# One-hot matrices of the second keys kept in DRAM between two halves of an expert layer, and a new split of the row gathers

## The chip, the cores and the metric

The kernel runs on one core of a Trainium2 chip. The metric is the device time of one execution in microseconds, lower is better. A measurement is the median of several runs.

## What is computed

A trunk of two layers over 512 tokens of width 1024. Each layer has a mixer (gMLP gating beside stick-breaking attention), which the change does not touch, and then PEER: each token picks 8 x 16 of 16384 single-neuron experts by two sets of 128 sub-keys and adds their outputs. Cut to that part:

```python
s1 = jnp.einsum('phd,kd->phk', q[:, :, 0], k1); s2 = jnp.einsum('phd,kd->phk', q[:, :, 1], k2)
v1, i1 = lax.top_k(s1, 16); v2, i2 = lax.top_k(s2, 16)
...                                   # top 16 of the pair sums
eid = jnp.take_along_axis(i1 * 128 + i2, top_pos, axis=-1)
g = jax.nn.softmax(top_s, axis=-1)
act = jax.nn.gelu(jnp.einsum('pd,phkd->phk', xb, u_tab[eid]))
return jnp.einsum('phk,phkd->pd', g * act, v_tab[eid])
```

## The kernel before

**Two ways through the experts.** Tokens 0 to 383 (ND = 384) are computed densely: for each of the 128 blocks of 128 experts (block b holds the experts with first key b) TensorE multiplies the whole block. The last 128 tokens are computed by gathers: for each of 128 picks, one indirect DMA fetches a row of `u` for each token, VectorE takes its dot product with the token (L825), and later 128 gathers of `v` rows are added up with their weights (L833). That is 256 gathers of 512 KB a layer. Each gather has one of three buffers `grow_` (L820 on): GpSimd may issue gather n+3 only when VectorE is done with gather n.

**Items and stages.** A *u item* is 24 matmuls of 384 columns (L128 to L130, into one of two PSUM banks `u0`, `u1`, which alternate from item to item), then a gelu on ScalarE (L536 and L539). A *v item* is 18 matmuls of 512 columns into `acc`. `PLAN` at the top of the file sets four stages: 32 u items (blocks 32 to 63; the first 32 blocks run earlier, beside other work), 64 v items, 64 u items, 64 v items. They are called **u1, v1, u2 and v2** here. PLAN also gives each stage its gathers: 2, 100, 64, and the rest, 90.

**One-hots.** The routing weights are made dense by matmuls. For 16 tokens at a time, `onehots(c, tg)` builds on VectorE `oa`, the one-hot of the second key (L758), `om`, that of the first key in the half c (L761), and `ob`, `om` times the weight in two parts (L765). Then `spread` (L773, L774) multiplies `oa` by `ob`, 8 tokens (16 short matmuls) at a time, and `weigh` moves the result to SBUF: VectorE L788 where the gelu of the block is known, ScalarE L790 where not. There are 24 such groups in u1 (c = 0) and the same 24 again in u2 (c = 1); `oa` does not depend on c. In u2 a spread writes into the `u` bank that the u item before it has used, so it has to wait until ScalarE has read that bank (L536, L539).

**Order.** All of this is under a manual schedule: each engine works through its instructions in the order in which the code is written. `run` calls, for the item i of a stage, `meanwhile(i)` when two of its eight k steps (six matmuls) are issued:

```python
fresh = [spread(*hot.pop(0)) for _ in range(steps[i][1])]
while late: late.pop(0)()
for part in fresh: weigh(*part)
...
if todo and len(hot) <= TG // TB and ...: hot.extend(onehots(*todo.pop(0)))
due = min(steps[i][2], len(left))
if due: gather(left.pop(0))
prepare(i + LOOK)
for _ in range(due - 1): gather(left.pop(0))
```

`prepare(i + 2)` loads the weights of the item after the next: a DMA on SyncE's queue (L121) into one of two buffers `raw` (u items) or one of the pool `wide` (v items), a copy to `hi` on ScalarE (L114), and `lo` = raw - hi on VectorE (L117). The item's own gelu on ScalarE comes behind this `hi`. The pool `wide` has four buffers of 512 KB; in u1 and u2 they hold two pairs of `oa` and `ob`.

Of the kernel before, what the change touches and what calls it, by code (L numbers as in the profile page):

```python
# [10 lines left out]
F32 = mybir.dt.float32  # L11
F32R = mybir.dt.float32r
F16 = mybir.dt.float16
# [4 lines left out]
OP = mybir.AluOpType  # L18
# [3 lines left out]
P = 128  # L22
L = 2
S = 512
D = 1024
KD = D // P
NTT = S // P
NDT = 3
ND = NDT * P
GT = 3  # L30
NH = 8
NK = 128
# [5 lines left out]
CH = NK // 2  # L38
NS2 = 11
NS1 = CH - NS2  # L40
TG = 16
SUB = 2
# [17 lines left out]
HEAD = 1  # L60
MID = 2
PLAN = [("u", range(FIRST, CH), 1, 2),
        ("v", [*range(NS1, CH), *range(NS1)], 0, 100),
        ("u", range(CH, NK), 1, 64),
        ("v", range(CH, NK), 0, 2 * P)]


# [1 line left out]
def trunk(ctx: ExitStack, tc: tile.TileContext, x, rows1, rows2, ada, w_qk, w_row, w_o, wq, kt, wst,  # L69
          vnorm, fnorm, ut, u_rows, v_rows, out):  # L70
    nc = tc.nc
    V, A, G, T = nc.vector, nc.scalar, nc.gpsimd, nc.tensor
# [1 line left out]
    cp = ctx.enter_context(tc.tile_pool(name="const", bufs=1))  # L74
    st = ctx.enter_context(tc.tile_pool(name="stream", bufs=2))

    xd = ctx.enter_context(tc.tile_pool(name="xd", bufs=1, space=bass.MemoryType.DRAM)).tile([NTT, P, D], F32, name="xd")
    held = {}

    def open_xs():  # L80
# [412 lines left out]
    def peer(l):  # L493
        with tc.tile_pool(name="pe", bufs=1) as pe, \
# [7 lines left out]
            i2t = pe.tile([P, ND], F16, name="i2t")  # L502
# [229 lines left out]
            with tc.tile_pool(name="gp", bufs=1) as gp, ExitStack() as psc:  # L732
                iot = gp.tile([P, P, SUB], F16, name="iot")
# [17 lines left out]
                def by_key(rows, n):  # L751

                    return rows.rearrange("p (g i) -> p g i", i=SUB)[:, :, None, :].to_broadcast([P, TG // SUB, n, SUB])

                def onehots(c, tg):
                    ts = slice(tg * TG, (tg + 1) * TG)
                    oa = gp.tile([P, TG // SUB, P, SUB], F16, name="wide", bufs=4)
                    V.tensor_tensor(oa, iot[:, None].to_broadcast([P, TG // SUB, P, SUB]), by_key(i2t[:, ts], P),  # L758
                                    OP.is_equal)
                    m = gp.tile([P, TG // SUB, CH, SUB], F16, name="om", bufs=1)  # L760
                    V.tensor_tensor(m, iot[:, None, c * CH:(c + 1) * CH].to_broadcast([P, TG // SUB, CH, SUB]),  # L761
                                    by_key(i1t[:, ts], CH), OP.is_equal)
                    ob = gp.tile([P, 2, TG // SUB, CH, SUB], F16, name="wide", bufs=4)
                    for part in range(2):
                        V.tensor_tensor(ob[:, part], m, by_key(gt[:, part, ts], CH), OP.mult)  # L765
                    return [(c, tg * TG + q * TB, oa, ob) for q in range(TG // TB)]
# [73 lines left out]
                def run(steps):  # L840
# [6 lines left out]
                    def meanwhile(i):  # L847
                        fresh = [spread(*hot.pop(0)) for _ in range(steps[i][1])]
                        while late:
                            late.pop(0)()  # L850
                        for part in fresh:
                            weigh(*part)
                        if i + 1 < len(steps) and len(steps[i + 1][0]) > 2:
                            close[i + 1] = steps[i + 1][0][2]()
                        if todo and len(hot) <= TG // TB and todo[0][0] <= steps[min(i + 1, len(steps) - 1)][4]:
                            hot.extend(onehots(*todo.pop(0)))
                        due = min(steps[i][2], len(left))
                        if due:
                            gather(left.pop(0))
                        prepare(i + LOOK)  # L860
                        for _ in range(due - 1):
                            gather(left.pop(0))

                    for i in range(LOOK):
                        prepare(i)
                    hot.extend(onehots(*todo.pop(0)))
                    for i in range(len(steps)):
                        w = ready.pop(i) + close.pop(i, ())
# [20 lines left out]
                for side, bs, spreads, gathers in PLAN:  # L889
                    items = [(u_item if side == "u" else v_item)(b) for b in bs]  # L890
                    chunk += spreads
                    n, g0, n0 = len(items), 0, 0
# [89 lines left out]
```

## Time and profile before

| | |
|---|---|
| median of 3 runs | 3146.86 us (3141.15 to 3151.80) |
| profiled execution, its own time | 3151.26 us |
| its span | 3149.6 us |
| TensorE matmul busy | 2988.5 us, 95% |
| VectorE busy | 2485.8 us, 79% |
| ScalarE busy | 1167.8 us, 37% |
| GpSimd busy | 798.6 us, 25% |
| u2 in the first layer | about 1010 to 1318 us |
| u2 in the second layer | about 2554 to 2858 us |

Busy shares are means over stages with different limits, so the stages are read one by one: how long a stage took, how many matmuls it held, and how long the same matmuls take in a stretch without a wait. The ends of matmuls in the records are modelled, so the pace is read from their starts and counts.

### The profile page before, as it was taken

How to read it: one execution, taken by the hardware profiler on the slowest of the kernel's cores; microseconds unless marked ns; L12 is line 12 of the kernel's file. 1: busy time of each engine (PE TensorE's matmuls, PEld its weight loads, DVE VectorE, ACT ScalarE, POOL GpSimd, SP SyncE). 2: the span in 40 equal slices, each digit the busy share in tenths (PEclk: the TensorE clock that was granted, in tenths of full speed). 3: DMA queues.
4: the chain of work that ended last, by engine and by line, in shares of the span. 5: the costliest groups of instructions: out<-in, count | busy, mean ns of one | idle time of the engine just before them, and what ended most of it. 6: DMA issues, size and time to landing. Idle time of an engine off the chain costs nothing. (4 is left out here: it accounts for less than half of the span.)

```text
span 3149.6 us, 47135 instructions
## 1 busy us (share of the span) xinstructions
PE 2988.5 (95%) x17532; PEld 2612.1 (83%) x17532; DVE 2485.8 (79%) x4951; ACT 1167.8 (37%) x2016; POOL 798.6 (25%) x584
## 2 busy tenths in 40 slices
PE   5988999999999999999999999999999999999998
PEld 4777888998777999977778888889987789998776
DVE  7687798797778889777853558969887888997787
ACT  3263333333333433333343633324333334333332
POOL 0000000003545323244500000000055543333452
PEclk8999999999999999999999999999999999999999
DMA  8746233337888666688832032333388876667885
GB/s 301 253 159 208 88 101 113 109 108 257 304 305 283 248 215 238 228 313 302 287 117 94 3 107 90 105 114 114 129 307 307 306 268 235 227 233 271 320 304 202
DMA packets 178840, 651.45 MB, mean 207 GB/s; under 512 B 19850, under 2 KB 20274, under 8 KB 178610
## 3 DMA queue, kind: packets, MB, share of 16 engines
q1 hardware_dynamic: 104018, 378.14, 35.8%
q0 software_dynamic: 73728, 268.47, 22.7%
q8 instruction: 137, 2.24, 0.3%
q10 hardware_dynamic: 864, 1.84, 0.2%
q14 instruction: 93, 0.76, 0.1%
HBM read 642.08 MB, written 6.29 MB: 206 GB/s over the span
## 5 line engine op out<-in xcount | busy, mean ns | idle before, releaser
L128 PE MATMUL u<-hh,hi 128*128 128x384 f32 x1920 | 665.1, 346 | 20.1 <-ACT act L539 17.3
L130 PE MATMUL u<-hh,lo 128*128 128x384 f32 x1920 | 648.2, 338 | 5.5 <-DVE lo L117 5.5
L129 PE MATMUL u<-hl,hi 128*128 128x384 f32 x1920 | 647.2, 337 | 0.0
L130 PE MATMUL acc<-hi,hl 128*128 128x512 f32 x1536 | 607.8, 396 | 32.8 <-DVE hl L117 32.5
L129 PE MATMUL acc<-lo,hh 128*128 128x512 f32 x1536 | 602.8, 392 | 7.0 <-DVE lo L117 6.9
L128 PE MATMUL acc<-hi,hh 128*128 128x512 f32 x1536 | 601.1, 391 | 0.0
L117 DVE TENSOR_TENSOR lo<-raw,hi 128x1024 fp32r<-128x1024 f32 x350 | 426.6, 1221 | 193.3 <-ACT hi L114 192.5
L114 ACT ACTIVATE hi<-raw 128x1024 fp32r<-128x1024 f32 x352 | 372.5, 1059 | 521.4 <-PE b L129 132.1
L114 ACT ACTIVATE hh<-act 128x384 fp32r<-128x384 f32 x256 | 134.4, 525 | 680.6 <-PE acc L129 677.5
L128 PEld LDWEIGHTS u<-hh,hi 128*128 128x128 f32 x1920 | 363.9, 190 | 24.7 <-ACT act L539 18.6
L130 PEld LDWEIGHTS acc<-hi,hl 128*128 128x128 f32 x1536 | 289.5, 188 | 113.3 <-DVE hl L117 54.3
L130 PEld LDWEIGHTS u<-hh,lo 128*128 128x128 f32 x1920 | 363.5, 189 | 6.6 <-DVE lo L117 6.6
L129 PEld LDWEIGHTS u<-hl,hi 128*128 128x128 f32 x1920 | 364.4, 190 | 1.4
L129 PEld LDWEIGHTS acc<-lo,hh 128*128 128x128 f32 x1536 | 289.7, 189 | 75.3 <-DVE lo L117 15.1
L128 PEld LDWEIGHTS acc<-hi,hh 128*128 128x128 f32 x1536 | 289.9, 189 | 57.9
L117 DVE TENSOR_TENSOR lo<-wide,hi 128x1024 fp32r<-128x1024 f32 x232 | 283.0, 1220 | 2.2 <-ACT hi L114 2.2
L114 ACT ACTIVATE hi<-wide 128x1024 fp32r<-128x1024 f32 x232 | 242.7, 1046 | 0.0
L117 DVE TENSOR_TENSOR hl<-act,hh 128x384 fp32r<-128x384 f32 (+1 forms) x272 | 152.8, 562 | 17.6 <-ACT hh L114 16.3
L128 PE MATMUL b<-hh,hi 128*128 128x512 f32 x336 | 132.5, 395 | 21.0 <-DVE hh L116 21.0
L234 DVE SCALAR_TENSOR_TENSOR aw<-aw,crow 128x1024 f32<-128x1024 f32 x96 | 116.9, 1222 | 44.9 <-DMA aw<-in_ada 44.6
L536 ACT ACTIVATE gu<-u 128x384 f32<-128x384 f32 (+23 forms) x186 | 63.7, 343 | 199.0 <-PE u L130 199.0
L129 PE MATMUL b<-hl,hi 128*128 128x512 f32 x336 | 131.1, 392 | 0.5 <-DVE hl L117 0.5
(1519 smaller groups left out, 5071.2 us busy)
## 6 DMA issues: line engine op xcount, KB each, us to landing
raw<-in_ut SPq DMA_DIRECT2D x240, 512.0 KB, 3.5
wide<-in_v_rows SPq DMA_DIRECT2D x232, 512.0 KB, 5.0
aw<-in_ada SPq DMA_DIRECT2D x96, 512.0 KB, 4.3
raw<-in_wq SPq DMA_DIRECT2D x32, 512.0 KB, 3.4
raw<-in_w_row SPq DMA_DIRECT2D x24, 512.0 KB, 4.2
raw<-in_v_rows SPq DMA_DIRECT2D x24, 512.0 KB, 6.0
raw<-in_w_qk SPq DMA_DIRECT2D x16, 512.0 KB, 3.5
raw<-in_w_o SPq DMA_DIRECT2D x16, 512.0 KB, 4.0
```

The lines of the kernel that those rows point to most:

```text
L114: A.activation(dst_hi, src, AF.Copy)
L117: sub.tensor_tensor(dst_lo, src, dst_hi.bitcast(F32), OP.subtract)
L128: T.matmul(o, lh, rh, start=first, stop=False)
L129: T.matmul(o, lh, rl, start=False, stop=False)
L130: T.matmul(o, ll, rh, start=False, stop=last)
L234: V.scalar_tensor_tensor(aw, aw, 1.0, crow[0], op0=OP.mult, op1=OP.mult, accum_out=modc[:, l, j:j + 1])
L536: A.activation(g[:, :n], pu[:, :n], AF.Gelu_apprx_tanh)
```

## The change

In u1 the finished `oa` is also written to a DRAM tile `od`, by a DMA on GpSimd's queue. In u2 `oa` is not computed again but loaded from `od`, by a DMA on SyncE's queue, at the place in the program where L758 stood. PLAN gives 94 gathers to v1 instead of 100 and 76 to u2 instead of 64; v2 has 84 left instead of 90.

```diff
-        ("v", [*range(NS1, CH), *range(NS1)], 0, 100),
-        ("u", range(CH, NK), 1, 64),
+        ("v", [*range(NS1, CH), *range(NS1)], 0, 94),
+        ("u", range(CH, NK), 1, 76),
         ("v", range(CH, NK), 0, 2 * P)]
...
+    od = dram.tile([ND // TG, P, TG * P], F16, name="od")
...
                     oa = gp.tile([P, TG // SUB, P, SUB], F16, name="wide", bufs=4)
-                    V.tensor_tensor(oa, iot[:, None].to_broadcast([P, TG // SUB, P, SUB]), by_key(i2t[:, ts], P),
-                                    OP.is_equal)
+                    flat = oa.rearrange("p g n i -> p (g n i)")
+                    if c == 0:
+                        V.tensor_tensor(oa, iot[:, None].to_broadcast([P, TG // SUB, P, SUB]), by_key(i2t[:, ts], P),
+                                        OP.is_equal)
+                        G.dma_start(out=od[tg], in_=flat)
+                    else:
+                        nc.sync.dma_start(out=flat, in_=od[tg])
```

SyncE's queue in u2, before: weight loads alone, each behind VectorE's release of its `raw` buffer (lines of the changed file are 3 to 8 higher).

```order
L121 DMA raw_9264<-in_ut 128x1024 [waits DMAHW7_49,DVE_49]
L121 DMA raw_9322<-in_ut 128x1024 [waits DMAHW0_49,DVE_49]
L121 DMA raw_9387<-in_ut 128x1024 [waits DMAHW1_49,DVE_49]
L121 DMA raw_9445<-in_ut 128x1024 [waits DMAHW2_49,DVE_49]
L121 DMA raw_9513<-in_ut 128x1024 [waits DMAHW3_49,DVE_49]
```

The same queue at the same place, after. `wide_9226`, `wide_9390` and `wide_9516` are three of the `oa` tiles.

```order
L767 DMA wide_9226<-od_64 128x2048 [waits DMAHW4_49,PE_49]
L124 DMA raw_9236<-in_ut 128x1024 [waits DMAHW1_49,DVE_49]
L124 DMA raw_9274<-in_ut 128x1024 [waits DMAHW2_49,DVE_49]
L124 DMA raw_9335<-in_ut 128x1024 [waits DMAHW4_49,DVE_49]
L767 DMA wide_9390<-od_64 128x2048 [waits DMAHW0_49,PE_49]
L124 DMA raw_9400<-in_ut 128x1024 [waits DMAHW5_49,DVE_49]
L124 DMA raw_9458<-in_ut 128x1024 [waits DMAHW6_49,DVE_49]
L767 DMA wide_9516<-od_64 128x2048 [waits DMAHW3_49,PE_49]
```

A load of `oa` now stands ahead of every second or third weight load and waits for TensorE: its buffer is that of the `oa` two groups earlier, whose last spread has to be over. All but the first two of the 24 loads of a layer have that wait. Between them stand two and three weight loads by turns.

ScalarE in u2, after, around the weight tile `raw_9400`, which stands behind `wide_9390` above. `u1_9362` is the bank of the item in which that load is issued, `u1_9434` the spread of the next item.

```order
L798 ACTIVATE act_2277<-u0_9369 128x53x8
L117 ACTIVATE hi_9402<-raw_9400 128x1024 [waits DMAHW0_49]
L539 ACTIVATE gu_9424<-u1_9362 128x48 [waits PE_49,Activation_49]
L542 ACTIVATE act2_2507<-u1_9362 128x336
L798 ACTIVATE act2_2507<-u1_9434 128x2x8 [waits DVE_49]
```

Nothing moved here: the copy of the weights stood ahead of the item's gelu before, too. What is new is what the weight tile stands behind on SyncE's queue.

GpSimd in u1, after: 14 stores now stand ahead of the first gather and 10 more ahead of the second; before, the gathers stood alone.

```order
L765 DMA od_64<-wide_5701 128x2048 [waits DMASW4_49,DVE_49]
L765 DMA od_64<-wide_5784 128x2048 [waits DMASW5_49,DVE_49]
L830 DMA grow__5847<-in_u_rows,ids_2272 128x1024 [waits DMASW6_49]
L765 DMA od_64<-wide_5925 128x2048 [waits DMASW7_49,DVE_49]
L765 DMA od_64<-wide_6008 128x2048 [waits DMASW0_49,DVE_49]
```

What moved: the first gather is issued behind the stores and no longer at the start of the stage.

## Rows read from the trace of the kernel before

**Rows 1.** Windows: v1, u2 and v2 (62 items) of both layers; the head names columns.

```profile
core 0: us, PE busy (x) PEld busy (x) DVE busy (x) ACT busy (x) POOL busy (x), PEclk, DMA share, GB/s
...
733.50:1010.10 276.60, 267.42 (x1154) 214.99 (x1153) 218.50 (x322) 93.95 (x128) 141.28 (x98) 1.00 0.85 300
1010.10:1317.90 307.80, 298.69 (x2306) 289.06 (x2305) 266.17 (x408) 116.51 (x244) 98.41 (x68) 0.99 0.64 231
1317.90:1594.90 277.00, 262.28 (x1126) 210.38 (x1125) 216.04 (x221) 93.66 (x129) 127.04 (x88) 0.99 0.81 287
2279.30:2553.90 274.60, 265.99 (x1153) 215.14 (x1152) 220.30 (x324) 93.66 (x127) 141.39 (x99) 1.00 0.86 303
2553.90:2858.00 304.10, 297.07 (x2305) 287.37 (x2304) 264.97 (x406) 117.03 (x244) 96.25 (x67) 1.00 0.65 233
2858.00:3128.20 270.20, 261.59 (x1126) 211.87 (x1126) 217.34 (x222) 93.89 (x129) 127.88 (x88) 0.99 0.83 296
```

**Rows 2.** Windows without a wait: 16 v items, 5 u items with 4 spreads, 3 u items.

```profile
733.40:798.70 65.30, 65.30 (x290) 54.11 (x289) 51.91 (x76) 24.04 (x33) 33.64 (x23) 1.00 0.85 297
1036.60:1059.80 23.20, 23.20 (x186) 22.57 (x185) 19.01 (x33) 10.18 (x23) 6.24 (x5) 1.00 0.62 231
1305.40:1317.90 12.50, 12.50 (x74) 12.50 (x74) 6.04 (x8) 4.73 (x7) 0.00 (x0) 1.00 0.41 158
```

**Rows 3.** Windows of L833 alone (one operation a gather), v2 of both layers.

```profile
1318.00:1582.00 264.00, 115.43 (x90) 0.99 0.83 295
2858.00:3115.00 257.00, 115.40 (x90) 0.99 0.84 303
```

**Rows 4.** Windows of L825 alone (two instructions a gather), v1 of the first layer.

```profile
734.00:1018.00 284.00, 123.01 (x200) 1.00 0.85 299
```

**Rows 5.** Timeline of VectorE in v2: start, duration, what it waited for.

```profile
1393.29 1.28 DVE L833 SCALAR_TENSOR_TENSOR hrow<-grow__12977,gg,hrow 128x1024 f32<-128x1024 f32 x1 [2.47 <-DMA grow__12977<-in_v_rows,ids]
```

**Rows 6.** Line L822, the gathers, in v2 of the first layer: who waited for them, landing.

```profile
  DVE hrow L833: 54.2, 48
...
DMA to landing us min/median/max: 4.7/6.6/9.1
```

**Rows 7.** Groups of VectorE by line: count, busy us, mean ns, idle before.

```profile
L117 DVE TENSOR_TENSOR lo<-raw,hi 128x1024 fp32r<-128x1024 f32 x350 | 426.6, 1221 | 193.3 <-ACT hi L114 192.5
...
L758 DVE TENSOR_TENSOR wide<-iot,i2t 128x2048 f16<-128x2048 f16 x96 | 116.7, 1216 | 1.9 <-POOL iot L734 1.9
```

**Rows 8.** Timelines of TensorE, then ScalarE, at a late weight tile in u2.

```profile
1073.46 0.33 PE L128 MATMUL u<-hh,hi 128*128 128x384 f32 x1
...
1075.64 0.19 PE L773 MATMUL u<-wide 128*128 128x64 f16 x1 [0.97 <-ACT act L539]
...
1074.10 1.06 ACT L114 ACTIVATE hi<-raw 128x1024 fp32r<-128x1024 f32 x1 [2.45 <-DMA raw<-in_ut]
...
1075.17 0.42 ACT L539 ACTIVATE act<-u 128x312 f32<-128x312 f32 x1
```

**Rows 9.** Timelines of TensorE and VectorE: an item's start, and its spread's release.

```profile
1171.94 0.33 PE L128 MATMUL u<-hh,hi 128*128 128x384 f32 x1
...
1173.68 0.50 DVE L788 SCALAR_TENSOR_TENSOR act<-u,act 128x88 f32<-128x88 f32 x2 [0.74 <-PE u L774]
```

**Rows 10.** Timeline of SyncE's queue: two loads issued back to back.

```profile
516.90 0.33 SPq L121 DMA_DIRECT2D raw<-in_ut  x1
517.32 0.38 SPq L545 DMA_DIRECT2D plain<-in_ut  x1
```

**Rows 11.** The page's DMA issues: KB each, median us from issue to landing.

```profile
raw<-in_ut SPq DMA_DIRECT2D x240, 512.0 KB, 3.5
...
raw<-in_v_rows SPq DMA_DIRECT2D x24, 512.0 KB, 6.0
...
plain<-in_ut SPq DMA_DIRECT2D x16, 512.0 KB, 4.7
```

**Rows 12.** Tile `raw` on SyncE's queue in u2 of the first layer: landing.

```profile
DMA to landing us min/median/max: 3.4/3.7/7.4
```

More of the change, by code (lines that the diff above doesn't have):

```diff
@@ L75, in trunk @@
     st = ctx.enter_context(tc.tile_pool(name="stream", bufs=2))
-    xd = ctx.enter_context(tc.tile_pool(name="xd", bufs=1, space=bass.MemoryType.DRAM)).tile([NTT, P, D], F32, name="xd")
+    dram = ctx.enter_context(tc.tile_pool(name="xd", bufs=1, space=bass.MemoryType.DRAM))
+    xd = dram.tile([NTT, P, D], F32, name="xd")
+    od = dram.tile([ND // TG, P, TG * P], F16, name="od")
     held = {}
```

## The prediction

> **What bounds the kernel now.** TensorE is busy 95% of the span, so I read first where it waits all the same. That takes a pace. In stretches without a wait 16 v items take 65.3 us, 4.08 us each, and 3 u items 12.5 us, 4.17 us each; five u items with four spreads take 23.2 us, so a spread adds (23.2 - 5 x 4.17) / 4 = 0.59 us [rows 2]. Against that pace the stages of [rows 1] show their waits. v1 should take 64 x 4.08 = 261.1 us and takes 276.6 and 274.6: 15.5 and 13.5 us of waits. The first 62 items of v2 should take 253.0 us and take 277.0 and 270.2: 24.0 and 17.2 us. u2 should take 64 x 4.17 + 48 x 0.59 = 295.2 us and takes 307.8 and 304.1: 12.6 and 8.9 us. Together that is 92 us, and all that this change can win lies in it.
>
> The waits of the v stages are those of the gathers. VectorE stands still until a gather has landed, 54.2 us in 48 times in v2 of one layer [rows 6], once 2.47 us in [rows 5]. With three buffers a gather can only be issued when the third before it is used up, and it takes 6.6 us to land [rows 6]; so the gathers have a period of their own, 264 / 90 = 2.93 us and 257 / 90 = 2.86 us in v2 [rows 3], 284 / 100 = 2.84 us in v1 [rows 4]. TensorE's pace asks for more: v2 spreads its 90 gathers over 58 items, one per 58 x 4.08 / 90 = 2.63 us, and v1 one per 261.1 / 100 = 2.61 us. VectorE works in order, so what stands behind the waiting operation (`lo` and the split of the activations) comes late to TensorE.
>
> **The v stages, fewer gathers.** v2 with 84 gathers: 84 x 2.93 = 246 us instead of 264, and 84 x 2.86 = 240 instead of 257, each 17 us less. The demand becomes one per 236.6 / 84 = 2.82 us, close to the period. I take 17 us in the first layer and, since only 17.2 us of waits are there and not all of them need be gathers, 14.5 in the second. v1: six gathers fewer at 2.84 us are 17 us, more than the waits; the demand is one per 2.78 us, still a little under 2.84, so I leave 1.5 to 2 us standing and take 13.5 and 12. Sum: **-57 us**. Bounds: the whole of the waits, -70; and half of it, -28, if the waits come from two gathers that fall on one item and not from the mean rate.
>
> **VectorE in u2.** 24 operations of 1.216 us go [rows 7], 12 gathers of 1.28 us [rows 5] come: 29.2 - 15.4 = 13.8 us less for each layer. That can win no more than the waits of u2, 12.6 and 8.9 us, which are part of the sum below, as I build u2 anew from the pace.
>
> **The loads on SyncE's queue in u2.** This is the term that decides. The order shows that 22 of the 24 loads of a layer wait for TensorE, for the last spread of the group two earlier, and that this spread belongs to the very item in which the load is issued. The weight tile of the item after the next is behind it on the same queue. On ScalarE the copy of that tile to `hi` stands ahead of the item's own gelu, and the next item's spread needs this gelu, since it writes the bank that the gelu reads. So there is a loop: spread, load, weight tile, `hi`, gelu, next spread. Before, the weight tile had only to wait for VectorE's release of its buffer.
>
> The loop has a length. From an item's start to the release by its spread: 1173.68 - 1171.94 = 1.74 us [rows 9]. From the load's issue to that of the weight tile behind it: 0.42 us [rows 10]. So the tile is issued 2.16 us after the item's start; call its landing T. From the landing to the next spread: in the one place where the trace shows the end of this loop, a weight tile was late, `hi` began at 1074.10 as it landed, the gelu followed and the spread began at 1075.64, 1.54 us after [rows 8]. Without a wait the next item starts 4.17 + 0.59 = 4.76 us after the first and its spread six matmuls later (6 / 24 x 4.17 = 1.04), at 5.80. The wait is 2.16 + T + 1.54 - 5.80 = **T - 2.1 us**. Spreads stand in four of five items, and a load is in the second and the fourth of them: after the first of the two loads the next item has a spread (11 times a layer), after the other it has none (11 times). Then the bank has time, and what is late is the item after the next, which starts at 4.76 + 4.17 = 8.93 and needs `lo` at its third matmul, at 9.28; `lo` is there at 2.16 + T + 1.06 [rows 8] + 1.22 [rows 7], so the wait is T - 4.8, if positive.
>
> T is the landing of the second of two loads of 512 KB issued together. Alone such a load lands in 3.5 us over the whole run and 3.7 in u2 [rows 11, 12]. As the second of a pair, `plain` behind `raw` where there are no gathers, it takes 4.7, and the last `v` tiles, the same among gathers, take 6.0 [rows 11]. u2 lies between: it moves 231 GB/s [rows 1], with 24 loads and 12 gathers more (18.9 MB) some 265, against 300 in v1. I take T = 5.6, nearer to the upper row. Then the waits are 3.5 and 0.8 us, 11 x 4.3 = 47 us a layer; with T = 4.7 they are 11 x 2.6 = 29, with T = 6.0 11 x (3.9 + 1.2) = 56. Of the old waits I leave 1 us. u2 then takes 295.2 + 47 + 1 = 343 us instead of 307.8 and 304.1, **+74 us** for both layers (+38 with T = 4.7, +92 with 6.0).
>
> The Trainium skill, in "DMA: Bandwidth & Descriptors", section "Anatomy of one DMA", fits a transfer as 2.0 us and its bytes at 436 GB/s: an estimate of 3.2 us for 512 KB alone, where the trace has 3.5, and of 2.0 + 2.4 - 0.42 = 4.0 us for the second of a pair, where it has 4.7. With that price u2 would lose only about 22 us a layer in the loop and the whole sum would be about -34 us.
>
> **The stores in u1.** A store reads `oa` while TensorE's spreads do. The buffer is wanted again two groups later, over 11 us (24 groups in 32 items of at least 4.17 us), and the longest landing of a DMA of GpSimd is 9.1 us [rows 6]; they are hidden. The first gather of a layer now comes behind 14 stores, so VectorE may stand up to 6.6 us [rows 6] in one item of u1; weights are made two items (8.3 us) ahead, which covers it: 0, at worst 13 us for both layers.
>
> **Sum.** -57 + 74 = +17 us. On the profiled execution (3151.3 us) that is 3168; it lies 4.4 us above the median, so on the median of 3146.9 I get **3164 us**. A measurement of this kernel can tell about 0.3%, 9.4 us, from no change.
>
> **Rivals.** (1) *A short loop.* The pair lands in 4.7 us or less, as without gathers: +38 - 57 = -19 us, 3128. For it speaks that single loads in u2 land in 3.7 us, hardly more than elsewhere [rows 12]; against it the longest of them, 7.4, and the added traffic. This is the other side: from T = 5.2 down the v stages win more than u2 loses (11 x (2 x 5.2 - 6.9) = 38 us a layer, u2 334, +56). The skill's price, in the paragraph above, is an extreme of it. (2) *The gathers' waits stay.* They come from bunching, and the v stages give only 28 us: +46, 3193. For it: items with two gathers still stand beside items with one. Against it: the period hardly changes between v1 and v2, whatever the operation. With T = 6.0 and the full 57 us it is +35, 3182. (3) *The loads hide.* The change does what it seems to say: `oa` costs nothing in u2, and VectorE's 13.8 us take u2 down to about 297: -17 - 57 = -74, 3073. It would need SyncE to let later loads pass a waiting one, which the order gives no room for. That the store or load is not made at all is excluded by the order.
>
> **Chances.** Forecast 0.45 (3137 to 3181), rival 1 0.22, rival 2 or T of 6.0 and more 0.28, rival 3 0.05. Of the forecast a good part, 0.18, lies within 0.3%, some of rival 1 as well. Faster 0.25, same 0.20, slower 0.55. The range of 3126 to 3196 reaches to both bounds of T with 57 us and to rival 2; outside are rival 3, the skill's extreme and the two bad ends together.
>
> **What the profile after would show.** Right: v1 and v2 near 263 and 258 us (62 items), u2 near 343, with TensorE's L781 (the spread) waiting for ScalarE's gelu L542 some 11 times a layer by 2 to 4 us, and ScalarE's `hi` waiting for `raw`; a `raw` behind an `od` load landing in 5 to 6 us. Wrong: spreads that wait for nothing (rival 3), waits under 2.5 us (rival 1), or v stages that still show 8 us and more of waits each (rival 2). If u1 grows, the stores cost what I set at nothing.

## The result and the profile after

The changed kernel takes **3274.57 us** (median of 4 runs, 3266.93 to 3285.12) against 3145.55 for the kernel before beside it: a ratio of 1.0403, 95% interval 1.0383 to 1.0423. It is slower by 129 us. The forecast was 3164 us, 17 more than before, with a range up to 3196; the sign was the likelier one, the size was more than seven times too small.

The profiled execution took 3266.93 us with a span of 3265.2, 115.6 us more than the span before. The windows of the changed kernel, by stage, say where (columns as in [rows 1]; the first line is u1, then v1, u2, v2 of the first layer, then v1, u2, v2 of the second):

```profile
572.60:732.90 160.30, 159.96 (x1537) 155.39 (x1537) 142.89 (x221) 62.97 (x174) 17.77 (x28) 1.00 0.57 201
732.90:996.20 263.30, 262.39 (x1154) 216.00 (x1153) 211.14 (x311) 93.96 (x127) 135.18 (x93) 1.00 0.86 307
996.20:1393.40 397.20, 327.67 (x2305) 311.46 (x2304) 254.84 (x401) 115.82 (x244) 96.39 (x79) 0.91 0.66 224
1393.40:1649.80 256.40, 255.24 (x1126) 210.12 (x1125) 208.74 (x215) 93.66 (x128) 119.17 (x82) 1.00 0.83 298
...
2333.60:2599.90 266.30, 263.84 (x1154) 215.61 (x1153) 212.81 (x313) 93.85 (x127) 135.85 (x93) 1.00 0.86 305
2599.90:2988.80 388.90, 325.13 (x2305) 309.39 (x2304) 253.56 (x399) 116.24 (x244) 94.36 (x79) 0.92 0.67 229
2988.80:3246.30 257.50, 256.09 (x1127) 209.97 (x1126) 209.44 (x216) 93.83 (x129) 119.72 (x82) 1.00 0.83 298
```

Against [rows 1] the four v stages have won 13.3 + 8.3 + 20.6 + 12.7 = 55 us; v1 and v2 now stand 2 to 5 us above what their matmuls need (261.1 and 253.0). u2 has lost 89.4 and 84.8, together 174. And in u2 the granted clock, 0.99 and 1.00 before, is 0.91 and 0.92.

The waits of u2 in the first layer, by engine, line and releaser (total us, times, longest):

```profile
ACT hi L117 <- DMA raw<-in_ut: 130.7, 25, 7.5
DVE lo L120 <- ACT hi L117: 109.0, 47, 6.2
...
PE u L781 <- ACT act L542: 59.5, 17, 5.8
...
PE u L131 <- ACT act L542: 6.6, 7, 1.7
...
PE u L133 <- DVE lo L120: 2.8, 10, 1.0
```

That is the loop that the prediction described: the weight tile late, `hi` (L117) behind it, the gelu behind that, and the spread (L781) waiting for the gelu. One pass through it, first SyncE's queue, then ScalarE, then TensorE (start, duration, and in brackets how long the engine had been idle and for what):

```profile
1108.96 0.33 SPq L767 DMA_DIRECT2D wide<-od  x1
1109.38 0.86 SPq L124 DMA_DIRECT2D raw<-in_ut  x2
...
1116.55 1.06 ACT L117 ACTIVATE hi<-raw 128x1024 fp32r<-128x1024 f32 x1 [6.47 <-DMA raw<-in_ut]
1117.51 0.25 ACT L539 ACTIVATE gu<-u 128x112 f32<-128x112 f32 x1
1117.66 0.39 ACT L542 ACTIVATE act<-u 128x272 f32<-128x272 f32 x1
...
1112.84 0.34 PE L133 MATMUL u<-hh,lo 128*128 128x384 f32 x1
1118.10 0.21 PE L781 MATMUL u<-wide 128*128 128x64 f16 x1 [4.92 <-ACT act L542]
...
1118.92 0.67 PE L131 MATMUL u<-hh,hi 128*128 128x384 f32 x1
```

The load of `oa` is issued at 1108.96, as soon as the spread of its own item is over; the weight tile follows at 1109.38 and lands at about 1116.55, when `hi` starts: 7.2 us. 1.55 us later the spread begins. TensorE had stopped after six matmuls and stood for 4.92 us. What follows is slow as well. The 16 matmuls of the spread take 1118.92 - 1118.10 = 0.82 us instead of the usual 0.59, and the matmul after them lasts 0.67 us where the one before the wait lasted 0.34. Windows of the same pass tell why (the last three columns are granted clock, share of the DMA engines, GB/s):

```profile
1106.90:1111.90 5.00, 4.95 (x42) 4.71 (x41) 4.55 (x10) 1.81 (x4) 1.07 (x2) 1.00 0.98 297
1112.00:1118.00 6.00, 1.18 (x7) 0.95 (x6) 0.94 (x3) 1.45 (x3) 0.94 (x1) 0.78 0.89 347
1118.10:1119.00 0.90, 0.90 (x17) 0.90 (x16) 0.90 (x2) 0.00 (x0) 0.00 (x0) 0.50 0.04 14
1119.00:1121.00 2.00, 2.00 (x9) 2.00 (x8) 1.57 (x5) 1.38 (x2) 0.07 (x1) 0.50 0.00 0
1121.00:1122.00 1.00, 1.00 (x5) 1.00 (x4) 0.94 (x1) 0.03 (x1) 0.87 (x1) 0.50 0.00 0
1122.00:1123.60 1.60, 1.60 (x10) 1.60 (x9) 1.43 (x3) 0.00 (x0) 0.00 (x0) 0.93 0.58 105
1123.70:1128.40 4.70, 4.70 (x42) 4.54 (x40) 3.26 (x7) 1.02 (x3) 0.94 (x1) 1.00 0.81 274
```

Two things stand here. While TensorE is stopped the granted clock falls, and when it runs again it does so at 0.50, the lower level of 1.2 GHz, until about 1122; so a wait costs more than its own length. In the first layer's u2 TensorE's own waits (the three PE lines above) come to 69 us, while the stage is 397.2 - 295.2 = 102 us longer than its work; the other 33 us are lost while TensorE runs.

The other thing is the traffic, which comes in a burst: the DMA engines are busy for 0.9 and more while the loop waits for its tile, with 347 GB/s, and move nothing in the 3 us after it. The mean of u2, 224 GB/s, is lower than before (231) and hides that.

Over both layers, read from the records of the 44 loads that wait, in the two kinds of the prediction: in the 22 where the next item has a spread, the tile behind the load lands 6.93 us after its issue (19 with a record), and the next item is 6.76 us longer than its 4.76 us of work. In the other 22 the tile takes 5.80 us (again 19 with a record), and the two items after are longer by 0.71 + 1.23 = 1.94 us. A pair of them costs 8.7 us, and 11 x 8.7 = 95.7 us is the whole of u2's distance from its work: 295.2 + 95.7 = 391 us, measured 397.2 and 388.9.

### The profile page after: what moved, and what is told of

It reads as the page before. It is cut to its first block, busy times and chain, and to the rows that moved or that the text cites. A ratio compares the mean times of both kernels' runs of the same rounds, so it can differ in the third digit from the quotient of the medians.

```text
span 3265.2 us, 47318 instructions
## 1 busy us (share of the span) xinstructions
PE 3026.2 (93%) x17532; PEld 2654.6 (81%) x17532; DVE 2431.9 (74%) x4903; ACT 1166.0 (36%) x2016; POOL 788.9 (24%) x632
## 5 line engine op out<-in xcount | busy, mean ns | idle before, releaser
L131 PE MATMUL u<-hh,hi 128*128 128x384 f32 x1920 | 683.1, 356 | 31.7 <-ACT act L542 30.7
L133 PE MATMUL u<-hh,lo 128*128 128x384 f32 x1920 | 661.7, 345 | 5.0 <-DVE lo L120 5.0
L132 PE MATMUL u<-hl,hi 128*128 128x384 f32 x1920 | 660.4, 344 | 0.0
L117 ACT ACTIVATE hi<-raw 128x1024 fp32r<-128x1024 f32 x352 | 372.3, 1058 | 733.9 <-DMA raw<-in_ut 305.1
L133 PE MATMUL acc<-hi,hl 128*128 128x512 f32 x1536 | 599.5, 390 | 3.0 <-DVE hl L120 3.0
L131 PE MATMUL acc<-hi,hh 128*128 128x512 f32 x1536 | 597.8, 389 | 0.0
L131 PEld LDWEIGHTS u<-hh,hi 128*128 128x128 f32 x1920 | 376.4, 196 | 41.3 <-ACT act L542 37.4
L133 PEld LDWEIGHTS u<-hh,lo 128*128 128x128 f32 x1920 | 374.0, 195 | 11.4 <-DVE lo L120 11.4
L132 PEld LDWEIGHTS u<-hl,hi 128*128 128x128 f32 x1920 | 376.1, 196 | 1.4
L117 ACT ACTIVATE hh<-act 128x384 fp32r<-128x384 f32 x256 | 134.5, 525 | 634.8 <-PE acc L132 634.8
L131 PEld LDWEIGHTS acc<-hi,hh 128*128 128x128 f32 x1536 | 288.3, 188 | 59.1
L117 ACT ACTIVATE hi<-wide 128x1024 fp32r<-128x1024 f32 x232 | 243.0, 1047 | 0.7 <-DMA wide<-in_v_rows 0.7
L782 PEld LDWEIGHTS <-wide 128*128 128x128 f16 x1536 | 106.2, 101 | 117.1 <-issue 116.0
L781 PE MATMUL u<-wide 128*128 128x64 f16 x768 | 67.5, 204 | 114.1 <-ACT act L542 113.5
L131 PE MATMUL b<-hh,hi 128*128 128x512 f32 x336 | 132.7, 396 | 20.7 <-DVE hh L119 20.7
```

The costliest lines, as they stand in the source:

```text
L117: A.activation(dst_hi, src, AF.Copy)
L131: T.matmul(o, lh, rh, start=first, stop=False)
L132: T.matmul(o, lh, rl, start=False, stop=False)
L133: T.matmul(o, ll, rh, start=False, stop=last)
L781: T.matmul(pg[:, i], oa[:, g, :, j], ob[:, 0, g, :, j], start=True, stop=False)
L782: T.matmul(pg[:, i], oa[:, g, :, j], ob[:, 1, g, :, j], start=False, stop=True)
```

## The experiments

My theory after this reading: u2 loses its time by the place of the load's wait on SyncE's queue (held up by its own item's spread, with the weight tile behind it), by the gathers that make the pair land late, and by the clock. The rivals: it is the added traffic itself, or the twelve gathers.

**The new split alone.** The kernel before, with 94 and 76 gathers.

```diff
-        ("v", [*range(NS1, CH), *range(NS1)], 0, 100),
-        ("u", range(CH, NK), 1, 64),
+        ("v", [*range(NS1, CH), *range(NS1)], 0, 94),
+        ("u", range(CH, NK), 1, 76),
```

> Only the split of the gathers is changed (94, 76, 84); the one-hots are computed twice as in the kernel before. If the v stages' waits are those of the gathers' period, v1 and v2 take what they take in the changed kernel (263 to 266 and 256 to 258 us for 62 items) and u2, with 15.4 us more of VectorE's work, 304 to 323: the whole 3080 to 3120. If the v stages won for another reason (the prefetched first gathers, the stores), they stay at 270 to 277 and the whole at 3145 or above.

Measured: 3098.30 us, ratio 0.9835 (0.9819 to 0.9852). v1 took 264.9 and 268.2, v2 262.4 and 260.5, a gain of 42 us in these four windows, and u2 with twelve gathers more 307.0 and 306.2, where it had 307.8 and 304.1. So twelve gathers in u2 cost next to nothing by themselves (1.3 us in the two layers), although `oa` is still computed there: the added VectorE work that the one-hots were stored to make room for had room already. Three of the four v windows are some us longer than was expected from the changed kernel.

**The stored keys alone.** The changed kernel with the old split.

```diff
-        ("v", [*range(NS1, CH), *range(NS1)], 0, 94),
-        ("u", range(CH, NK), 1, 76),
+        ("v", [*range(NS1, CH), *range(NS1)], 0, 100),
+        ("u", range(CH, NK), 1, 64),
```

> Only the one-hots are stored and loaded; the gathers are split as in the kernel before (100, 64, 90). The v stages go back to 275 to 277 and 270 to 277 us. Theory of the queue order, with the length of the loop set by the traffic beside it: with 12 gathers fewer u2 stays near 375 to 390 us, the whole 3300 to 3330. If the 12 gathers more were the cause of u2's growth, u2 is back at 295 to 310 and the whole at 3130 to 3150.

Measured: 3298.15 us, ratio 1.0472 (1.0453 to 1.0490). u2 took 382.5 and 376.5, 147 us more than before for the two, and the v stages, with 277.8, 277.0, 272.5 and 271.9, stayed where they were. The loss is wholly that of the loads. With the split on top u2 loses another 27 us (397.2 + 388.9 - 382.5 - 376.5), which the twelve gathers do not cost without the loads: they make the loop longer, since they fly beside the tile that it waits for.

**The load behind the weight tiles.** The same loads, the same traffic, the same buffers, only issued behind `prepare`.

```diff
-                        nc.sync.dma_start(out=flat, in_=od[tg])
+                        loads.append((flat, od[tg]))
...
                         prepare(i + LOOK)
+                        while loads:
+                            flat, kept = loads.pop(0)
+                            nc.sync.dma_start(out=flat, in_=kept)
```

> The load of oa is issued on the same queue one place later, behind the weight tile of the item after the next; nothing else changes. Theory of the queue order (the weight tile waits behind a load that waits for TensorE): u2 falls from 397 and 389 us to 296 to 308 each, the v stages stay as in the changed kernel, the whole near 3085 us (3145.6 less 55 in the v stages and some 5 in u2). Rival, the added traffic itself (24 loads and 12 gathers more in u2 slow every weight tile): u2 stays above 370 us, the whole above 3240.

Measured: 3102.28 us, ratio 0.9849 (0.9825 to 0.9872), 172 us below the change as made. u2 took 312.5 and 309.5, somewhat above the 296 to 308 expected. In its waits the same lines are short (u2 of the first layer, columns as above):

```profile
ACT hi L117 <- DMA raw<-in_ut: 49.2, 26, 4.7
...
PE u L781 <- ACT act L542: 11.3, 13, 1.7
```

Traffic and number of loads are those of the change, so neither is the cost by itself; the place on the queue is. The load still waits there for the spread of its own item, but what stands behind it now is the tile of an item later. The waits are not all gone: this kernel only equals the new split alone, with its 24 operations fewer on VectorE.

**The load on GpSimd's queue.** One word changed.

```diff
-                        nc.sync.dma_start(out=flat, in_=od[tg])
+                        G.dma_start(out=flat, in_=od[tg])
```

> The load of oa goes to GpSimd's queue, at the same place in the program; it still waits for the spread. Queue order: no weight tile is behind it, only the next gather, which has three buffers of slack: u2 296 to 320 us, the whole 3085 to 3125. Added traffic as the cause: u2 above 370, the whole above 3240.

Measured: 3246.36 us, ratio 1.0317 (1.0300 to 1.0334), u2 374.9 and 373.4. The expectation failed. The loop was not broken but moved to another queue. Waits of u2 in the first layer, then GpSimd and VectorE around one load:

```profile
POOL wide L767 <- PE u L782: 183.6, 22, 10.9
...
PE u L131 <- ACT act L798: 36.4, 12, 4.6
```

```profile
1112.12 0.57 POOL L767 DMA_DIRECT2D wide<-od  x1 [8.57 <-PE u L782]
1112.99 0.96 POOL L830 DMA_INDIRECT grow__10100<-in_u_rows,ids  x1 [0.30 <-issue]
...
1118.33 1.23 DVE L833 SCALAR_TENSOR_TENSOR grow__10100<-grow__10100,hrow 128x1024 f32<-128x1024 f32 x1 [2.75 <-DMA grow__10100<-in_u_rows,ids]
```

GpSimd stands 8.57 us before it may issue the load, and the gather that could have been issued in that time comes behind it, at 1112.99. VectorE then waits for the gather, the operations behind it come late, and TensorE waits for ScalarE's part of the weighing (L798) where it waited for the gelu. That wait is 36 of the 80 us by which this u2 exceeds its work; where the rest goes stays open. I had asked what the load holds up on SyncE and not what it would hold up on GpSimd.

**No gathers in u2.** One execution, and of it only u2 is read: v2 takes all the remaining gathers and is long for that reason.

```diff
-        ("u", range(CH, NK), 1, 76),
+        ("u", range(CH, NK), 1, 0),
```

> The changed kernel with no gathers in u2 (94, 0, 160); only u2 is read, v2 becomes long. Theory: the weight tile behind a load lands 6.9 us after its issue (19 of the first kind in the changed kernel, 5.8 of the second kind) because gathers are in flight beside it; without them it lands in 4.6 to 5.0, as the second of a pair without gathers, the wait at the spread falls from 6.8 to about 2.6 to 3 us plus what the clock takes, and u2 to 325 to 345 us. Rival: the three loads that SyncE issues in a row make the 6.9; then it stays above 6.3 and u2 above 375.

Measured: u2 338.6 and 339.7 us. A load, the tile behind it and `hi` at its landing, then the two windows of u2:

```profile
1063.35 0.33 SPq L767 DMA_DIRECT2D wide<-od  x1
1063.76 0.86 SPq L124 DMA_DIRECT2D raw<-in_ut  x2
...
1067.85 1.06 ACT L117 ACTIVATE hi<-raw 128x1024 fp32r<-128x1024 f32 x1 [3.56 <-DMA raw<-in_ut]
```

```profile
995.30:1333.90 338.60, 310.77 (x2305) 300.54 (x2305) 165.72 (x290) 117.16 (x243) 2.82 (x2) 0.96 0.41 144
2731.10:3070.80 339.70, 310.19 (x2305) 298.99 (x2304) 167.70 (x292) 116.75 (x243) 4.66 (x3) 0.96 0.41 146
```

The tile is there 4.1 us after its issue; over the 44 pairs the time from the issue to the start of `hi` has a median of 4.5 us, between 4.1 and 6.4. The same load, and a third one as close behind, takes 6.9 with the gathers where the next item has a spread, 5.8 in the other kind. So the loop stands without gathers too, 44 us a layer above the work, and they make up the other half, 54 us, with all that they bring: the traffic, and 76 operations on VectorE.

**TensorE kept busy in the wait.** 80 products of 128 x 128, whose results nobody reads, stand ahead of the spread where the next item's spread will have to wait, so that TensorE works in a part of the wait.

```diff
                         if k == MID and meanwhile is not None:
+                            for _ in range(busy.pop(0) if busy else 0):
+                                T.matmul(pu[:, ND:], identb, identb, start=False, stop=False, skip_group_check=True)
                             meanwhile()
...
+                            if todo[0][0] == 1 and len(steps[i][0]) == 2 and steps[i + 1][1]:
+                                busy.append(FILL)
                             hot.extend(onehots(*todo.pop(0)))
```

> The changed kernel with 80 short matmuls (128 columns, into unused columns of the item's bank) ahead of the spread of each item that follows a load with a spread behind it; they take the place of TensorE's idle time. Theory: of the 6.8 us lost there, 1.9 are not waiting but the granted clock, which is 0.50 for some 3.7 us after the idle time; with TensorE kept busy it stays near 1.00 and u2 falls by 15 to 22 us a layer, the whole to 3230 to 3245. Rival: the clock does not depend on that idle time, or the matmuls cost what they save: 3265 to 3300.

Measured: 3257.68 us, ratio 1.0332 (1.0297 to 1.0366), where the change as made has 1.0403 (1.0383 to 1.0423). The windows of u2 in both layers, and the wait for the weight tile in the first:

```profile
997.80:1374.60 376.80, 356.15 (x3186) 337.65 (x3186) 254.61 (x403) 115.80 (x244) 97.20 (x79) 1.00 0.70 238
2590.80:2974.80 384.00, 358.61 (x3185) 340.81 (x3184) 254.41 (x401) 115.88 (x244) 97.25 (x79) 0.99 0.68 233
```

```profile
ACT hi L118 <- DMA raw<-in_ut: 131.0, 26, 7.3
```

The late tile is as late as in the change (131.0 us against 130.7), and 80 x 11 = 880 matmuls a layer were added, and still u2 is shorter, by 20 us in the first layer and 5 in the second; the granted clock is back at 1.00 and 0.99. That shows the clock as a cost of its own. It does not show its whole size: the added matmuls can outlast the wait and then delay the spread, and why the second layer gains so much less was not found. The whole, 3257.68 us, lies between the two expectations, so the size was expected too large.

**A fifth buffer.** The pool `wide` with five buffers, paid for by building `om` in the second half of `ob`. The load then waits for a spread that is an item or more back.

```diff
-                    oa = gp.tile([P, TG // SUB, P, SUB], F16, name="wide", bufs=4)
+                    oa = gp.tile([P, TG // SUB, P, SUB], F16, name="wide", bufs=5)
...
-                    m = gp.tile([P, TG // SUB, CH, SUB], F16, name="om", bufs=1)
+                    ob = gp.tile([P, 2, TG // SUB, CH, SUB], F16, name="wide", bufs=5)
+                    m = ob[:, 1]
...
-                    ob = gp.tile([P, 2, TG // SUB, CH, SUB], F16, name="wide", bufs=4)
```

> The changed kernel with five buffers in the pool of the one-hots in place of four (the room comes from building om in the second half of ob): the load of oa keeps its place on SyncE's queue ahead of the weight tile, but its buffer is free two to three items earlier, so it does not wait for the spread of its own item. Queue order: the wait, not the place or the traffic, is the cost; u2 296 to 312 us, the whole 3080 to 3105. If the traffic of two loads side by side were the cost, u2 stays above 340.

Measured: **3088.91 us, ratio 0.9791** (0.9759 to 0.9823), which beats both kernels; only the last one below equals it. u2 in both layers, and its wait for the weight tile:

```profile
996.80:1295.20 298.40, 296.22 (x2305) 287.14 (x2304) 254.32 (x401) 117.08 (x244) 114.24 (x79) 1.00 0.82 301
2509.10:2807.30 298.20, 296.11 (x2306) 287.52 (x2306) 252.56 (x398) 115.68 (x244) 114.80 (x78) 1.00 0.82 299
```

```profile
ACT hi L117 <- DMA raw<-in_ut: 14.1, 10, 3.6
```

u2 is 3 us above its work, with the same 76 gathers and the same 24 loads at the same place in the program; the burst is gone (301 GB/s over the whole stage). Only what the tiles of the pool wait for has changed. That settles the cause: not the load, nor its place by itself, but a load at the head of a queue that waits for its own item.

**Five buffers without the loads.** The gain over the new split alone could be the buffer's. So the split with five buffers, and `oa` computed as before.

> The split of the gathers 94/76 and five buffers, with oa still computed on VectorE in u2 (no store, no load). If the gain of the five-buffer kernel with loads (0.979) over the new split alone (0.9835) comes from VectorE's 24 operations of 1.22 us, this one stays at the new split's time, ratio 0.983 to 0.986, u2 near 307 us a layer. If it comes from the fifth buffer itself, this one equals the five-buffer kernel with loads: 0.978 to 0.981, u2 near 299 us.

Measured: 3101.07 us, ratio 0.9857 (0.9826 to 0.9887), which is the split alone. u2:

```profile
998.40:1302.70 304.30, 298.30 (x2305) 287.72 (x2304) 277.91 (x422) 115.51 (x243) 115.86 (x78) 1.00 0.72 254
2512.70:2818.40 305.70, 298.68 (x2305) 287.76 (x2304) 279.44 (x424) 115.44 (x243) 116.83 (x79) 1.00 0.71 253
```

With the loads VectorE's busy time (the fourth column) falls from 278 to 254 us and u2 by 13 us for both layers (610.0 - 596.6). So the idea of the change is probably worth something, 13 us, once its queue is in order: the intervals of these two ratios just fail to meet, but those of the five-buffer kernel and of the split alone overlap. The fifth buffer alone gives 3 us (613.2 - 610.0), within what runs differ.

**More gathers still.** The five-buffer kernel with 90 gathers in v1, 84 in u2 and 80 in v2.

> The five-buffer kernel with loads and a further shift of gathers: 90 in v1, 84 in u2, 80 in v2. If the waits that are left in v2 (262 against 253 us of work) are of the gathers, v2 falls to about 257 and the ratio to 0.975 to 0.978; if u2 pays for its eight further gathers with new waits (now about 3 us a layer), u2 grows by 4 us a layer or more and the ratio is 0.979 to 0.983.

Measured: 3086.69 us, ratio 0.9805 (0.9778 to 0.9832). v2 falls to 254.8 in both layers and u2 rises to 306.2 and 305.9; what one wins the other loses. This further shift wins nothing.

## Why the prediction was wrong

*The v stages* were right: 57 us forecast, 55 measured. The period of the gathers was the right reading: in v2 after, 84 of them take 247.6 us, 2.95 us each, as in [rows 3], and with fewer of them the stage hardly waits for it. The rival that only 28 us would come falls. Some of the closeness is luck: stage by stage 13.5, 12, 17 and 14.5 were forecast and 13.3, 8.3, 20.6 and 12.7 measured, and other runs with this split won 42 to 53 us.

*The stores in u1* were right: u1 takes 160.3 and 159.9 us against 159.7 before.

*The loop* was right in its chain and in its fixed parts: issue 1.73 us after the item's start at the median (forecast 1.74), landing to spread 1.57 on the mean (forecast 1.54). The rival that the loads hide falls, and so does the short loop.

*What failed is the price of the loop*, 47 us a layer forecast, 95.7 measured. The difference of 48.7 has three parts:

- **T, the landing of the weight tile.** I took 5.6 us, between `plain` behind `raw` and the last `v` tiles [rows 11], because u2's mean traffic lay between theirs. It is 6.93 us where the next item has a spread, above the upper bound of 6.0: 11 x 1.33 = 15 us. The upper row was read wrongly. Of its 24 tiles only 8 are issued within 0.51 us of the load ahead of them; the seven of these with a record land in 5.9 to 10.0 us, median 6.95. The other 16 are issued 2.4 us or more after the load ahead, and 6.0 is the median of both sorts. One such group in the trace of before, and the landing of its two `raw` tiles:

```profile
961.53 0.33 SPq L121 DMA_DIRECT2D wide<-in_v_rows  x1
961.91 0.91 SPq L121 DMA_DIRECT2D raw<-in_v_rows  x2
...
DMA to landing us min/median/max: 6.0/7.0/8.0
```

  The mean of the stage was the wrong measure as well. In the pass shown above, loads and gathers fly together behind one event, at 347 GB/s; without gathers the tile takes a median of at most 4.5 us. The Trainium skill's fit in "DMA: Bandwidth & Descriptors", section "Anatomy of one DMA", by which I estimated 4.0 us, is given there for DMAs that GpSimd issues. For these loads, which SyncE issues, the traces do not agree with it: both figures, 4.5 and 6.93, lie above the estimate.
- **TensorE after the wait.** I wrote the wait as T - 2.1 us, as if TensorE went on afterwards at its old pace. With T = 6.93 that is 4.83, and the item lost 6.76: 1.93 us more, 11 x 1.93 = 21 us, which the filled waits show to be the clock, at least in part. The trace of before had shown it already, in a place that I passed over. Behind a wait of 2.2 us in u2 the granted clock is 1.00 for 1.5 us more and then 0.51 for 3.4 us, in which eleven matmuls take some 3.5 us instead of 11 x 4.17 / 24 = 1.9:

```profile
1126.80:1129.00 2.20, 0.05 (x1) 0.00 (x0) 1.17 (x4) 1.69 (x4) 0.94 (x1) 1.00 0.00 0
1129.00:1130.50 1.50, 1.46 (x22) 1.46 (x21) 1.50 (x5) 0.04 (x1) 0.00 (x0) 1.00 0.75 202
1130.50:1133.90 3.40, 3.40 (x12) 3.40 (x12) 1.75 (x2) 1.34 (x2) 0.94 (x1) 0.51 0.76 229
```

- **The second kind of load.** T - 4.8 with the measured 5.80 is 1.0 us, forecast 0.8, measured 1.94: 11 x 1.14 = 12.5 us. I had counted the wait for `lo` alone. In 13 of the 22 the item after the next waits at its first matmul: it writes the bank of the load's own item, whose gelu stands behind `hi` (0.4 to 1.7 us; the line of L131 above), and that makes the item right after the load longer, where I had set nothing. In 9 of them the spread that follows waits for a gelu too, 0.2 to 1.2 us. TensorE's waits come to some 1.1 of the 1.94 us; the other 0.8 are lost while it runs, and whether the clock is all of that stays open.

The range failed with them. Its upper end took T = 6.0 from the misread row and gave the clock no place, while every microsecond by which the loop is longer counts 22 times over the two layers in its first kind alone.

## What to carry to other kernels

A DMA that waits for a semaphore holds up all that stands behind it on its queue, on GpSimd as on SyncE: before a load is put on a queue, look at what it waits for, and give its tile one buffer more, so that it waits for something long past (here u2 of both layers took 786 us with four buffers and 597 with five). Price a wait by what is in flight at that moment and not by the mean of the stage, take the landing from transfers that are issued in the same way, and add what TensorE's clock costs after it. And try the parts of a change apart: the new split alone gave 1.65%, the stored keys alone lost 4.7%, and with the fifth buffer they gave 0.4 to 0.7% on top of the split, about as much as the intervals are wide.

## What was not expected of the hardware

After 4.92 us without a matmul TensorE ran at a granted clock of 0.50, 1.2 GHz, until about 1122, some 4 us after it had started again; the mean cost was 1.93 us on top of a wait of 4.83. After a wait of 2.2 us in the kernel before, the fall to 0.51 came only 1.5 us after the work had begun again. A weight tile of 512 KB as second behind a load on the same queue landed in at most 4.5 us (median) without gathers beside it and with them in 6.9 where the next item has a spread, 5.8 where it has none.
